# A decoder trunk on one Trainium2 core: first loads held and reordered, last product in three parts

## The chip, the cores and the metric

The kernel runs on one core of one Trainium2 chip. A core has a matrix engine (TensorE, PE in the profile; its weight loads are listed apart as PEld), a vector engine (VectorE, DVE), a scalar engine (ScalarE, ACT), a general engine (GpSimd, POOL) and a synchronisation engine (SyncE, SP), each with a queue of its own that it works through in order. Transfers between HBM and the on-chip memory SBUF are issued from an engine's queue (here SP's, after the change ACT's too) and carried out by 16 DMA engines. Matrix products land in PSUM, eight banks of 128 x 512 32-bit numbers.

The metric is the device time of one execution in microseconds (us), lower is better, given as the median over several runs.

## What is computed

Two decoder layers on a sequence of 256 tokens with width 2048, all in 32-bit floating point. Layer 0 mixes tokens with 16-head attention that carries a forget gate, layer 1 with dilated windows; each layer ends with an MLP of width 8192. Cut to what matters here:

```
for i in range(2):
    h = rms_norm(x, mix_norm_g[i])                      # y = x * rsqrt(mean(x*x) + eps) * g
    x = x + (fox_attention(h, ...) if i == 0 else dilated_attention(h, ...))
    h = rms_norm(x, mlp_norm_g[i])
    x = x + (relu(h @ mlp_w_up[i]) ** 2) @ mlp_w_down[i]
return x

def fox_attention(h, w_in, b_f, q_gain, k_gain, w_out):
    q, k, v, f = split(h @ w_in)                        # w_in is 2048 x (3*2048 + 16)
    ...
```

## The kernel before

**Tiles.** x lies in SBUF as four tiles `xt[n]` (x0 to x3 in the trace, L142) of 128 partitions x 2 token blocks x 512 columns, 512 KB each. Weights come in pieces of 256 rows x 512 columns, also 512 KB: `load` (L252) issues one transfer into a `raw` tile (5 buffers), `split` (L268) turns it into two tiles, `wh` (ACT copies it into the matrix engine's reduced 32-bit format, L279) and `wl` (DVE subtracts that copy from the original, L280), 5 buffers each. So every weight piece costs one transfer, one ACT cast and one DVE subtraction.

**Products.** `product` (L297) multiplies the normalised activations with one 2048 x 512 block of weights, 16 steps over the depth (k), for two blocks of 128 tokens. Each step is three passes per token block: `wh` with the high part of the activations (L308), `wl` with the high part (L309), `wh` with the low part (L310). Two steps use up one weight piece, so a block is eight pieces and 96 passes of 512 columns. After each piece `split` is called for the piece five further on.

**The norm.** The gain g of the norm is applied when x is transposed: `norm_chain` (L356) transposes four 128 x 128 blocks of x on PE into a PSUM tile `ptx` (L365), ACT writes `hT` = ptx times gain (L370), DVE writes the low part (L371). The factor rsqrt(mean) is put in after the product; its sum of squares is taken by ACT (`junk`, L381). The gains themselves are loaded as rows (`g_mix`, L128), transposed on PE and copied by DVE into `gain` (L135, L136).

**The start.** SP issues, in this order: the gains' rows, x0 in two halves of 256 columns for both token blocks, the weight pieces 0 and 1, x1, the pieces 2 and 3, x2, piece 4, x3, the gate's weights `wf` (2048 rows of 64 bytes, L160), and so on. PE begins with eight transposes of an identity matrix into an unused tile (`wake(8)`, L116), then transposes the gains and x0, then twelve more of the idle transposes (`wake(12)`), then the first product (q of heads 0 to 3). After it stand the gate's 32 passes (`pf`, L520), and the second product (k of heads 0 to 3). In the second product stand `pft` (L536) and `pc` (L565), small products of the gate's chain, which runs for the rest on DVE and ACT.

**What sets the order.** `Jobs` (L41) is a hand-made planner: a generator that yields a number waits for so many steps over k ("ticks"). `norm_chain` gets two such numbers, `wait` before its transposes and `later` before its sums of squares. `behind(...)` (L243) only places instructions after others in the order of issue; a real wait comes from the data (a semaphore).

**The end.** The last product adds `acc * rstd * rstd` to x on DVE per token block (`add_chain`, L687, L692), and `store` (L705) sends 256 KB for each from SP's queue.

```
        acc = [ps_acc.tile([P, NC], F32, tag="acc", name=f"acc{used[0]}_{t}") for t in range(NT)]
        for k in range(KC):
            ...
            for t in range(NT):
                ...
                nc.tensor.matmul(acc[t], ah[:, tok], hi, start=first, stop=False)
                nc.tensor.matmul(acc[t], ah[:, tok], lo, start=False, stop=False)
                issued["product"] = nc.tensor.matmul(acc[t], al[:, tok], hi, start=False, stop=last)
```

Of the kernel before, what the change touches and what calls it, by code (L numbers as in the profile page):

```python
# [9 lines left out]
F32 = mybir.dt.float32  # L10
# [3 lines left out]
ALU = mybir.AluOpType  # L14
# [3 lines left out]
P = 128  # L18
D = 2048
S = 256  # L20
NT = S // P
# [66 lines left out]
def trunk(ctx: ExitStack, tc, x, fox_w_in, fox_b_f, fox_q_gain, fox_k_gain, fox_w_out, dil_w_in,  # L88
# [68 lines left out]
    def more_constants():  # L157
        yield 6
        wf = work.tile([P, KC, FH], F32, tag="t2", name="wf")
        nc.sync.dma_start(wf, fox_w_in[0][:, 3 * D:3 * D + FH].rearrange("(c p) n -> p c n", p=P))  # L160
        nc.sync.dma_start(bf, fox_b_f.to_broadcast([P, FH]))
        qk_rows = gain_rows("g_qk", [fox_q_gain, fox_k_gain, dil_q_gain[0], dil_k_gain[0]])
        mlp_rows = gain_rows("g_mlp", [mlp_norm_g.rearrange(per_chunk, p=P)])
        di = distances()
# [78 lines left out]
    def behind(*instructions):  # L243
# [3 lines left out]
        return stack  # L247

    state = {"raw": 0, "split": 0}
    raws, splits = [], []  # L250

    def load():  # L252
        i = state["raw"]
        if i >= len(plan):
            return
        w, r, cols = plan[i]
        t = wpool.tile([P, RAW_SUB, NC], F32, tag="raw", name=f"raw{i}", bufs=RAW_BUFS)
        at = 0
        for c, width in cols:
            nc.sync.dma_start(  # L260
                t[:, :, at:at + width],
                w[r:r + RAW_SUB * P, c:c + width].rearrange("(c p) n -> p c n", p=P),
            )
            at += width
        raws.append(t)
        state["raw"] += 1

    def split():  # L268
        i = state["split"]
        per = RAW_SUB // W_SUB  # L270
        if i >= len(plan) * per:
            return
        if i % per == 0:
            load()
        raw = raws[i // per][:, (i % per) * W_SUB:(i % per + 1) * W_SUB, :]
        hi = wpool.tile([P, W_SUB, NC], F32R, tag="wh", name=f"wh{i}", bufs=W_BUFS)
        lo = wpool.tile([P, W_SUB, NC], F32R, tag="wl", name=f"wl{i}", bufs=W_BUFS)
        with behind(*(issued.get("n0", []) if i < 2 * W_BUFS else [])):
            nc.scalar.copy(hi, raw)  # L279
            nc.vector.tensor_sub(lo, raw, hi.bitcast(F32))  # L280
        splits.append((hi, lo))
# [15 lines left out]
    def product(keys, lhs, post):  # L297

        acc = [ps_acc.tile([P, NC], F32, tag="acc", name=f"acc{used[0]}_{t}") for t in range(NT)]
        for k in range(KC):  # L300
# [13 lines left out]
            jobs.tick()  # L314
        jobs.spawn(post(acc))

    def product_transposed(keys, both, banks, post):
# [38 lines left out]
    def norm_chain(tag, col, n, ssp, wait, later):  # L356
        yield wait
        for half in range(2):
            pr = n * 2 + half
            pt = ps_tp.tile([P, 2, S], F32, tag="tp", name=f"ptx_{tag}_{pr}")  # L360
            with behind(*([issued["product"]] if wait else [])):
                for i in range(2):
# [12 lines left out]
            jobs.done.add((tag, pr))  # L375
            yield min(wait, 1)
        yield later
        with behind(issued[tag, n * 2 + 1][0]):
            for t in range(NT):
# [307 lines left out]
    def add_chain(acc, n, then, ready, scale):  # L687
# [11 lines left out]
        yield 0  # L699

    def out_proj(keys, lhs, then=None, ready=None, scale=None):
        for n in range(NX):
            product(keys, lhs, lambda acc, n=n: add_chain(acc, n, then, ready, scale))

# [48 lines left out]

    first = normed("n0", 0, lambda n: (0, 1, 4, 8)[n], lambda n: 11 - 3 * n)

    def load_x(n):
        step = NC if n else NC // 2
        for c in range(0, NC, step):
            nc.sync.dma_start(xt[n][:, :, c:c + step], xv[:, :, n * NC + c:n * NC + c + step])

    def rest():
        load_x(2)
        yield 2
        split()
        load_x(3)
        while state["split"] - used[0] < W_BUFS:
            split()
            yield 1

    load_x(0)  # L770
    gain_columns("g_mix", mix_rows, 0)
    jobs.spawn(first(0))
    with behind(issued["transposed"]):
        wake(12)
    for i in range(4):
        split()
        if i == 1:
            load_x(1)
    for n in range(1, NX):
# [64 lines left out]
```

## Time and profile before

| | |
|---|---|
| median of three runs | 2198.79 us (2198.11 to 2200.05) |
| the profiled execution, its own time | 2198.39 us |
| span of its trace, first to last instruction | 2196.7 us |
| DVE / ACT busy | 1373.5 us / 1099.4 us |
| transfers from HBM | 421.70 MB, 193 GB/s over the span |
| x stored at the end | 8 transfers of 256 KB, median 5.5 us from issue to landing |

The lines of a timeline read: start in us from the span's start, duration, engine, line of the kernel, operation, written tile <- read tiles, shapes, number of merged instructions, and in brackets the idle time of that engine just before and what ended it. Names of tiles stand without buffer numbers. "SPq" is the work of SP's queue, here the issue of transfers, not the transfer itself. A duration of a PE row includes its pipeline's latency; how fast passes follow one another is read from the distance of their starts.

### The profile page before, as it was taken

To read this page: it belongs to the slowest core of one execution; us is meant where nothing else is said; L and a number is where in the kernel's file an instruction comes from. 1 tells how busy PE (TensorE), PEld (TensorE's weight loads), DVE (VectorE), ACT (ScalarE), POOL (GpSimd) and SP (SyncE) were. 2 spreads that over 40 slices of the span, in tenths; PEclk is the share of its full clock that TensorE was granted. 3 is DMA by queue.
4 is the path that set the end of the run, shared out by engine and by line. 5 is a ranking of instruction groups with operands and counts; after the bars stand their busy time and mean duration, and the time that the engine had idled before them with its cause. 6 is when DMAs were issued, how large, how long until landed. Compare 5 with 4: busy or idle time off the path is not lost.

```text
span 2196.7 us, 29876 instructions
## 1 busy us (share of the span) xinstructions
PE 2182.1 (99%) x11441; PEld 1938.2 (88%) x11441; DVE 1373.5 (63%) x1799; ACT 1099.4 (50%) x1516; POOL 48.2 (2%) x51
## 2 busy tenths in 40 slices
PE   8999999999999999999999999999999999999999
PEld 7888888998998998998888888888988988988988
DVE  6776686665565565565666766765655665665564
ACT  5555555554454454455555555555544544544442
POOL 1011000000000000000000000000000000000000
PEclk9999999999999999999999999999999999999999
DMA  7566545666666666665665565655656656656664
GB/s 233 163 184 179 177 170 196 197 202 203 202 201 203 202 202 204 201 202 194 192 190 182 173 192 172 193 173 192 202 204 203 202 203 204 200 203 202 201 211 143
DMA packets 248688, 425.76 MB, mean 194 GB/s; under 512 B 16793, under 2 KB 66529, under 8 KB 248545
## 3 DMA queue, kind: packets, MB, share of 16 engines
q1 hardware_dynamic: 248544, 423.86, 60.6%
q8 instruction: 89, 1.46, 0.3%
q14 instruction: 55, 0.44, 0.1%
HBM read 421.70 MB, written 2.10 MB: 193 GB/s over the span
## 4 chain that ended last, share of the span: by engine, by line
PE 95%; ACT 2%; DVE 2%; issue 1%; DMA 0%; SPq 0%; DVEq 0%; ACTq 0%
PE acc L310 20%; PE acc L308 20%; PE acc L309 20%; PE up_n3a_acc L329 5%; PE up_n1a_acc L329 5%; PE up_n3a_sc L329 3%; PE up_n1a_tp L329 3%; PE up_n3a_tp L329 3%; PE up_n1a_sc L329 3%; PE up_n1a_acc L333 3%; PE up_n3a_acc L333 3%; PE up_n1a_sc L333 1%; PE up_n3a_tp L333 1%; PE up_n1a_tp L333 1%; PE up_n3a_sc L333 1%; ACT wh L279 1%
## 5 line engine op out<-in xcount | busy, mean ns | idle before, releaser
L280 DVE TENSOR_TENSOR wl<-raw,wh 128x1024 fp32r<-128x1024 f32 x800 | 978.9, 1224 | 715.4 <-ACT wh L279 710.4
L279 ACT CAST wh<-raw 128x1024 fp32r<-128x1024 f32 x800 | 838.9, 1049 | 901.8 <-PE acc L310 546.3
L308 PE MATMUL acc<-wh,hT_n 128*128 128x512 f32 x896 | 346.2, 387 | 0.0
L309 PE MATMUL acc<-wl,hT_n 128*128 128x512 f32 x896 | 340.2, 380 | 0.0
L310 PE MATMUL acc<-wh,hT_n 128*128 128x512 f32 x896 | 339.8, 379 | 0.0
L308 PE MATMUL acc<-wh,aTh_n1a 128*128 128x512 f32 x512 | 194.5, 380 | 0.0
L309 PE MATMUL acc<-wl,aTh_n1a 128*128 128x512 f32 x512 | 194.0, 379 | 0.0
L310 PE MATMUL acc<-wh,aTl_n1a 128*128 128x512 f32 x512 | 194.0, 379 | 0.0
L308 PE MATMUL acc<-wh,aTh_n3a 128*128 128x512 f32 x512 | 194.0, 379 | 0.0
L309 PE MATMUL acc<-wl,aTh_n3a 128*128 128x512 f32 x512 | 194.0, 379 | 0.0
L310 PE MATMUL acc<-wh,aTl_n3a 128*128 128x512 f32 x512 | 194.0, 379 | 0.0
L310 PEld LDWEIGHTS acc<-wh,hT_n 128*128 128x128 f32 x896 | 169.4, 189 | 23.6
L308 PEld LDWEIGHTS acc<-wh,hT_n 128*128 128x128 f32 x896 | 169.6, 189 | 21.9 <-ACT wh L279 0.4
L309 PEld LDWEIGHTS acc<-wl,hT_n 128*128 128x128 f32 x896 | 169.6, 189 | 21.6 <-DVE wl L280 0.8
L329 PE MATMUL up_n3a_acc<-hT_n,wh 128*128 128x512 f32 x512 | 181.6, 382 | 0.0
L329 PE MATMUL up_n1a_acc<-hT_n,wh 128*128 128x512 f32 x512 | 181.6, 382 | 0.0
L333 PE MATMUL up_n3a_acc<-hT_n,wl 128*128 128x256 f32 x512 | 139.6, 273 | 0.0
L333 PE MATMUL up_n1a_acc<-hT_n,wl 128*128 128x256 f32 x512 | 139.6, 273 | 0.0
L309 PEld LDWEIGHTS acc<-wl,aTh_n3a 128*128 128x128 f32 x512 | 96.8, 189 | 13.8
L310 PEld LDWEIGHTS acc<-wh,aTl_n1a 128*128 128x128 f32 x512 | 96.8, 189 | 13.7
L310 PEld LDWEIGHTS acc<-wh,aTl_n3a 128*128 128x128 f32 x512 | 96.8, 189 | 13.7
L308 PEld LDWEIGHTS acc<-wh,aTh_n3a 128*128 128x128 f32 x512 | 96.8, 189 | 13.6
(721 smaller groups left out, 3159.9 us busy)
## 6 DMA issues: line engine op xcount, KB each, us to landing
raw<-in_mlp_w_up_dram SPq DMA_DIRECT2D x256, 512.0 KB, 4.3
raw<-in_mlp_w_down_dram SPq DMA_DIRECT2D x256, 512.0 KB, 3.9
raw<-in_fox_w_in_dram SPq DMA_DIRECT2D x96, 512.0 KB, 3.8
raw<-in_dil_w_in_dram SPq DMA_DIRECT2D x192, 256.0 KB, 3.0
raw<-in_fox_w_out_dram SPq DMA_DIRECT2D x32, 512.0 KB, 3.8
raw<-in_dil_w_in_dram SPq DMA_DIRECT2D x32, 512.0 KB, 3.6
raw<-in_dil_w_out_dram SPq DMA_DIRECT2D x32, 512.0 KB, 3.7
out_dram<-x SPq DMA_DIRECT2D x8, 256.0 KB, 5.5
```

Source lines behind the costliest of these rows:

```text
L279: nc.scalar.copy(hi, raw)
L280: nc.vector.tensor_sub(lo, raw, hi.bitcast(F32))
L308: nc.tensor.matmul(acc[t], ah[:, tok], hi, start=first, stop=False)
L309: nc.tensor.matmul(acc[t], ah[:, tok], lo, start=False, stop=False)
L310: issued["product"] = nc.tensor.matmul(acc[t], al[:, tok], hi, start=False, stop=last)
L329: issued["product"] = nc.tensor.matmul(banks[b], hi[:, i, col], in_turn(tokens.rearrange("p x s -> p (x s)"), P // 2), start=first, stop=last)
L333: nc.tensor.matmul(banks[b][:, 0:S], lo[:, i, col], in_turn(tokens[:, 0, :], P // 2), start=False, stop=False)
```

## The change

- x0 is loaded in two pieces by token block (whole rows of 512 columns) instead of two pieces by columns.
- Weight piece 0 is loaded in two halves from ACT's queue.
- The pieces 1 to 4 and x1 to x3 are issued in the order piece 1, x1, piece 2, x2, piece 3, x3, piece 4. Each is held by a small DVE memset into its destination, which is placed behind the copy that writes `gain`; so the transfer has to wait for that memset.
- Piece 0 is cast and subtracted in two halves, ahead of the first `hT`.
- Only x0's first two chunks are transposed before the first product; the second two stand inside it. `wake(12)` becomes `wake(6)`.
- The gate's weights, its bias and the other gains are loaded later, behind the last weight load; the sums of squares of the first norm are taken later (`later` is 13, 11, 9, 7 instead of 11, 8, 5, 2).
- In all norms, the sums of squares are placed behind the last cast issued, instead of behind the norm's last `hT`.
- The very last product (`last_product`) has three accumulators: token block 0 with 512 columns, token block 1 with 256 columns twice. For k below 8 the three take turns; then each runs its remaining steps alone, one after the other, and is added to x and stored as soon as it is done, the last one from ACT's queue.

```diff
     def more_constants():
-        yield 6
+        yield 9
         wf = work.tile([P, KC, FH], F32, tag="t2", name="wf")
-        nc.sync.dma_start(wf, fox_w_in[0][:, 3 * D:3 * D + FH].rearrange("(c p) n -> p c n", p=P))
-        nc.sync.dma_start(bf, fox_b_f.to_broadcast([P, FH]))
-        qk_rows = gain_rows("g_qk", [fox_q_gain, fox_k_gain, dil_q_gain[0], dil_k_gain[0]])
-        mlp_rows = gain_rows("g_mlp", [mlp_norm_g.rearrange(per_chunk, p=P)])
+        with behind(issued["load"]):
+            nc.sync.dma_start(wf, fox_w_in[0][:, 3 * D:3 * D + FH].rearrange("(c p) n -> p c n", p=P))
+            nc.sync.dma_start(bf, fox_b_f.to_broadcast([P, FH]))
+            qk_rows = gain_rows("g_qk", [fox_q_gain, fox_k_gain, dil_q_gain[0], dil_k_gain[0]])
+            mlp_rows = gain_rows("g_mlp", [mlp_norm_g.rearrange(per_chunk, p=P)])
...
+    def hold(first):
+        if "held" not in issued:
+            return ExitStack()
+        with behind(*issued["held"]):
+            nc.vector.memset(first, 0.0)
+        return behind(issued["load"])
...
-            nc.sync.dma_start(
-                t[:, :, at:at + width],
-                w[r:r + RAW_SUB * P, c:c + width].rearrange("(c p) n -> p c n", p=P),
-            )
+            src = w[r:r + RAW_SUB * P, c:c + width].rearrange("(c p) n -> p c n", p=P)
+            if i:
+                with hold(t[:, 0, 0:1]):
+                    issued["load"] = nc.sync.dma_start(t[:, :, at:at + width], src)
+            else:
+                for part in range(RAW_SUB):
+                    nc.scalar.dma_start(t[:, part, at:at + width], src[:, part, :])
...
-        if i % per == 0:
+        if i % per == 0 and state["raw"] <= i // per:
             load()
...
-        with behind(*(issued.get("n0", []) if i < 2 * W_BUFS else [])):
-            nc.scalar.copy(hi, raw)
-            nc.vector.tensor_sub(lo, raw, hi.bitcast(F32))
+        with behind(*([issued["gained"]] if i == 0 else issued.get("n0", []) if i < 2 * W_BUFS else [])):
+            for part in ([slice(0, 1), slice(1, 2)] if i < 1 else [slice(0, W_SUB)]):
+                issued["cast"] = nc.scalar.copy(hi[:, part, :], raw[:, part, :])
+                nc.vector.tensor_sub(lo[:, part, :], raw[:, part, :], hi[:, part, :].bitcast(F32))
...
+    def last_product(keys, lhs, ready):
+        parts = [(0, slice(0, NC)), (1, slice(0, S)), (1, slice(S, NC))]
+        acc = [ps_acc.tile([P, NC], F32, tag="acc", name=f"last{x}") for x in range(len(parts))]
+        begin = used[0]
+        steps = [(k, x) for k in range(KC // 2) for x in range(len(parts))]
+        steps += [(k, x) for x in range(len(parts)) for k in range(KC // 2, KC)]
+        for k, x in steps:
+            jobs.need(keys(k))
+            t, cols = parts[x]
+            hi, lo = (in_turn(w[:, k % W_SUB, :])[:, 0, cols.start // 2:cols.stop // 2, :]
+                      for w in splits[begin + k // W_SUB])
+            ah, al = lhs(k)
+            tok = slice(t * P, (t + 1) * P)
+            first, last = k == 0, k == KC - 1
+            to = acc[x][:, 0:cols.stop - cols.start]
+            nc.tensor.matmul(to, ah[:, tok], hi, start=first, stop=False)
+            nc.tensor.matmul(to, ah[:, tok], lo, start=False, stop=False)
+            nc.tensor.matmul(to, al[:, tok], hi, start=False, stop=last)
+            if last:
+                ready(to, t, cols)
+            if k < KC // 2 and x == len(parts) - 1:
+                if k % W_SUB == W_SUB - 1:
+                    split()
+                jobs.tick()
...
-            with behind(*([issued["product"]] if wait else [])):
+            with behind(*([issued["product"]] if "product" in issued else [])):
...
-            yield min(wait, 1)
+            yield 1
         yield later
-        with behind(issued[tag, n * 2 + 1][0]):
+        with behind(issued["cast"]):
...
+    def final_add(n, tag):
+        def ready(acc, t, cols):
+            at = halves(xt[n][:, t, :])[:, 0, :, cols.start // 2:cols.stop // 2]
+            sums = acc.rearrange("p (n h) -> p h n", h=2)
+            nc.vector.scalar_tensor_tensor(at, sums, rstd[tag, 2][:, t:t + 1], at, ALU.mult, ALU.add)
+            dst = out[0][t * P:(t + 1) * P, n * NC:(n + 1) * NC].rearrange("p (h n) -> p h n", h=2)
+            (nc.scalar if cols.start else nc.sync).dma_start(dst[:, :, cols.start // 2:cols.stop // 2], at)
+        return ready
+
     def out_proj(keys, lhs, then=None, ready=None, scale=None):
         for n in range(NX):
+            if ready is not None and n == NX - 1:
+                last_product(keys, lhs, final_add(n, scale))
+                continue
...
-    first = normed("n0", 0, lambda n: (0, 1, 4, 8)[n], lambda n: 11 - 3 * n)
+    first = normed("n0", 0, lambda n: (0, 2, 6, 10)[n], lambda n: (13, 11, 9, 7)[n])
 
     def load_x(n):
-        step = NC if n else NC // 2
-        for c in range(0, NC, step):
-            nc.sync.dma_start(xt[n][:, :, c:c + step], xv[:, :, n * NC + c:n * NC + c + step])
+        for t in range(NT) if n == 0 else [slice(0, NT)]:
+            with hold(xt[n][:, 0, 0:1]):
+                issued["load"] = nc.sync.dma_start(xt[n][:, t, :], xv[:, t, n * NC:(n + 1) * NC])
 
     def rest():
-        load_x(2)
-        yield 2
-        split()
-        load_x(3)
         while state["split"] - used[0] < W_BUFS:
             split()
             yield 1
 
     load_x(0)
-    gain_columns("g_mix", mix_rows, 0)
+    load()
+    gained = gain_columns("g_mix", mix_rows, 0)
+
+    issued["gained"] = gained
+    issued["held"] = [gained]
+    for what in (load, lambda: load_x(1), load, lambda: load_x(2), load, lambda: load_x(3), load):
+        what()
+    del issued["held"]
     jobs.spawn(first(0))
     with behind(issued["transposed"]):
-        wake(12)
-    for i in range(4):
-        split()
-        if i == 1:
-            load_x(1)
+        wake(6)
+    split()
     for n in range(1, NX):
         jobs.spawn(first(n))
     jobs.spawn(rest())
```

## The prediction, made before the changed kernel ran

> **What bounds the kernel now.** I read the page first, then the timeline of the start engine by engine, the busy times by stretch, and the end.
>
> ```profile
> span 2196.7 us, 29876 instructions
> PE 2182.1 (99%) x11441; PEld 1938.2 (88%) x11441; DVE 1373.5 (63%) x1799; ACT 1099.4 (50%) x1516; POOL 48.2 (2%) x51
> PE 95%; ACT 2%; DVE 2%; issue 1%; DMA 0%; SPq 0%; DVEq 0%; ACTq 0%
> ```
>
> The matrix engine is busy 99% of the time and carries 95% of the chain that ended last. It has only a start, a tail and a few stalls to give. The order in which both kernels are built shows that the change moves instructions before about 60 us and in the last product; between them only some sums of squares change places on ACT. So I reckon from the span's start to the first pass of the second product, and then the tail. SP's queue, PE and ACT at the start:
>
> ```profile
> 0.80 0.39 SPq L128 DMA_DIRECT2D g_mix<-in_mix_norm_g_dram  x1
> 1.25 0.93 SPq L759 DMA_DIRECT2D x<-in_x_dram  x2
> 2.22 0.98 SPq L260 DMA_DIRECT2D raw<-in_fox_w_in_dram  x2
> ...
> 8.39 0.79 SPq L160 DMA_DIRECT2D wf<-in_fox_w_in_dram  x1
> ```
>
> ```profile
> 4.07 1.11 PE L365 MATMUL ptx_n<-ident,x 128*128 128x128 f32 x4
> 6.77 1.09 PE L365 MATMUL ptx_n<-ident,x 128*128 128x128 f32 x4 [1.58 <-DMA x<-in_x_dram]
> 7.65 2.77 PE L116 MATMUL spare<-ident 128*128 128x128 f32 x12
> 10.38 1.22 PE L308 MATMUL acc<-wh,hT_n 128*128 128x512 f32 x2
> 11.64 0.52 PE L309 MATMUL acc<-wl,hT_n 128*128 128x512 f32 x1
> ...
> 12.64 0.60 PE L365 MATMUL ptx_n<-ident,x 128*128 128x128 f32 x4
> ```
>
> ```profile
> 2.09 0.20 ACT L105 ACTIVATE warm<-warm 128x1 f32<-128x1 f32 x1
> ...
> 12.46 1.05 ACT L279 CAST wh<-raw 128x1024 fp32r<-128x1024 f32 x1 [1.19 <-DMA raw<-in_fox_w_in_dram]
> 13.82 1.05 ACT L279 CAST wh<-raw 128x1024 fp32r<-128x1024 f32 x1 [0.32 <-DMA raw<-in_fox_w_in_dram]
> 14.78 0.47 ACT L370 ACTIVATE hT_n<-ptx_n,gain 128x256 fp32r<-128x256 f32 x1
> ...
> 21.74 1.04 ACT L279 CAST wh<-raw 128x1024 fp32r<-128x1024 f32 x1 [3.23 <-DMA raw<-in_fox_w_in_dram]
> ```
>
> The first product begins at 10.38. Two casts wait for pieces 2 and 3 until 12.46 and 13.82: one 512 KB transfer follows another in 1.36 us. Back from there in such steps, x1 landed at 11.1, piece 1 at 9.74, piece 0 at 8.38; x0's halves released PE at 4.07 and 6.77. So loads decide the start. The stretch behind it, and the passes that bound it:
>
> ```profile
> 10.37:42.81 32.44, 29.30 (x155) 24.01 (x155) 24.26 (x41) 22.83 (x43) 1.30 (x3) 1.00 0.89 273
> ```
>
> ```profile
> 27.11 0.63 PE L365 MATMUL ptx_n<-ident,x 128*128 128x128 f32 x4 [2.67 <-issue]
> ...
> 39.10 3.87 PE L520 MATMUL pf<-hT_n,wfs 128*32 128x256 f32 x32
> 42.81 0.38 PE L308 MATMUL acc<-wh,hT_n 128*128 128x512 f32 x1
> 43.03 0.38 PE L309 MATMUL acc<-wl,hT_n 128*128 128x512 f32 x1
> 43.24 0.38 PE L310 MATMUL acc<-wh,hT_n 128*128 128x512 f32 x1
> ```
>
> The second product begins at 42.81, 32.4 us after the first; PE's first figure, 29.30, is its busy time. The work in it: 96 passes at 0.2157 (42.81 to 43.24 are two steps) = 20.7; six groups of four transposes at 4 x 0.11 = 2.6 (0.60 less a latency of 0.27, over three steps); two small transposes of gains, estimated at 0.33 each beside such a group's 0.44; the gate 42.81 - 39.10 = 3.7. Together 27.7, so 4.7 us are stalls, some inside passes that the busy time counts. The largest is the 2.67 before 27.11. ACT stood there in its order: the cast of piece 5 at 21.74 had waited 3.23 for its load, and the high parts of x2 came behind it and the next cast. That load stood in SP's queue behind x3 and the gate's weights of 8.39.
>
> **The change, part by part.**
>
> *First loads.* Wanted first are x0 and the first half of piece 0. ACT issues that half at about 0.8, as its first instruction, the second half behind the table load and the warm-up, with an issue (0.39 as at 0.80) in front: 2.09 + 0.20 + 0.39 = 2.7. x0's first half before took 4.07 - 1.25 = 2.82 from issue to use. Its second piece is issued half of 0.93 later, at 1.72, and so wanted at 4.54; with the half piece of weights between, 1.36 / 2 = 0.68 more: 5.2. Bounds: 4.4 if ACT's transfer costs x0 nothing, and 7.2 if both pass as slowly as the first megabyte before (8.38, less 0.68 for the half not needed and 0.45 for the earlier issue). I take 5.2, nearest to the row at 4.07; whole rows double what the first transposes wait for.
>
> The Trainium skill, DMA: Bandwidth & Descriptors, "Issuing engines are not separate DMA queues", says that transfers issued from several engines run on the same 16 DMA engines and interleave; by that rule the 0.68 is due. No run of before, which issues everything from SP, can show it.
>
> *First pass.* Four transposes from 5.2 at 0.21 apart (2.77 less a latency of about 0.4, over eleven steps) leave PE at 6.1; six idle ones add 1.3: 7.3. The other path is not later: second half of piece 0 at 2.7 + 2.82 = 5.5, half a cast of 1.05, and hT 0.47, which waits for the transposes' end at about 6.3: 6.8. So the first pass starts at 7.3 (6.4 to 9.4 by x0's bounds), 3.1 earlier.
>
> *Held loads.*
>
> ```profile
> 4.17 0.19 DVE L136 COPY gain<-ps_g_mix 128x32 f32<-128x32 f32 x1 [0.53 <-PE ps_g_mix L135]
> ```
>
> `gain` is written at 4.36. Seven memsets of one column follow on DVE, ahead of its first subtraction; the nearest row, the one-column warm-up on ACT, took 0.20, so at most 1.4 us, ended at 5.8, before the first half's cast is subtracted for a pass at 7.3. Piece 1 is issued at about 4.5; of the loads in the first 50 us
>
> ```profile
> DMA to landing us min/median/max: 3.7/6.1/10.0
> ```
>
> the quickest took 3.7, so it lands at 8.2 (before 9.74), the next ones 1.36 apart: x1 9.6, piece 2 10.9, x2 12.3, piece 3 13.6, x3 15.0, piece 4 16.4, piece 5 17.7. PE needs 24 x 0.2157 + 0.88 = 6.1 us for one x tile and two pieces, the transfers 4.1, so loads stay ahead. Only piece 1 is tight: cast 1.05 and a subtraction of about as much behind 8.2, with an hT between, end at 11 to 11.5; PE wants them at 7.3 + 12 x 0.2157 + 0.44 = 10.3 at full pace. Piece 5 comes four us before the old 21.74, since the gate's weights now stand behind piece 8 (they are wanted only by the gate), so the 2.67 should go. Work to the second product's start is 20.7 + 7 x 0.44 (x0's second group now lies inside) + 0.33 + 3.7 = 27.8; the other gains' transpose moves into the second product, 0.3.
>
> *Pace.* Passes don't run at full speed at first. Four transposes took 1.11 and 1.09 early and 0.60 at 12.64; the two passes at 10.38 took 1.22. The granted-clock column says 1.00 in that stretch, so only durations show it; the turn lies near 11.7. If it comes after as much work without a break as before (6.77 to 11.7, 4.9 us), it falls at 5.2 + 4.9 = 10.1, and 10.1 - 7.3 at half pace costs 1.4. Ends: 0.4 (turn at 8.1) and 2.2 (turn at 11.7). With piece 1's wait of up to 0.8, partly in the same time, I put in 1.7 (0.9 to 3.0).
>
> Second product's start: 7.3 + 27.8 + 1.7 + 0.3 = 37.1 against 42.81: 5.7 gained.
>
> *Second product.*
>
> ```profile
> PE pc L565 <- DVE g_lf L562: 0.9, 1, 0.9
> ```
>
> `pc` waited 0.9 for the gate's chain on DVE. In the new order it stands 89 passes into that product, 19 us, instead of 54; the chain stands behind a subtraction whose buffer PE frees 17 passes, 3.7 us, earlier, time enough for a cast and a subtraction. The last sums of squares come behind a cast that PE frees 12 passes (2.6 us) in, and the product that needs them first starts 20 us in. I take 0.8 (0 to 1.0).
>
> *Tail.*
>
> ```profile
> 101.72 0.27 PE L469 MATMUL po_f<-pTh_f,fv0h 128*128 128x256 f32 x1
> 101.83 0.28 PE L469 MATMUL po_f<-pTl_f,fv0h 128*128 128x256 f32 x1
> 101.94 0.28 PE L469 MATMUL po_f<-pTh_f,fv0l 128*128 128x256 f32 x1
> ```
>
> ```profile
> 2192.13 1.41 DVE L692 SCALAR_TENSOR_TENSOR x<-acc,rstd_n,x 128x512 f32<-128x512 f32 x2 [10.00 <-PE acc L310]
> ...
> 2192.36 0.38 PE L310 MATMUL acc<-wh,aTl_n3a 128*128 128x512 f32 x1
> 2192.91 0.99 SPq L706 DMA_DIRECT2D out_dram<-x  x2
> ```
>
> ```profile
> L371 DVE SCALAR_TENSOR_TENSOR hT_n<-ptx_n,gain,hT_n 128x256 fp32r<-128x256 f32 x64 | 30.3, 482 | 16.2 <-ACT hT_n L370 15.8
> ```
>
> From the last pass's start to the span's end are 4.3 us: 0.38, the second of two additions of 0.70 on DVE, the store's issue and landing. After it: a 256-column pass ends 0.10 sooner; the addition takes 0.48 at most, as this row of 256 columns (-0.25), and starts free of the one before (-0.05); the store has half the bytes in twice as many pieces (0, from -0.2 to +0.3). Against it 96 passes at 0.11 stand for 48 at 0.2157: +0.2. Net -0.2 (-0.6 to +0.3). The casts of its last pieces are issued before the second half of k, so the quicker use of pieces there finds them ready; the third accumulator's buffer is freed by an addition about 0.4 before it is wanted.
>
> **Sum.** 5.7 + 0.8 + 0.2 = 6.7 off the profiled execution's 2198.39 (span and 1.7 around it), which lies 0.40 under the median of the runs: 2191.7 there, 2192.1 as a median.
>
> **The rivals.**
>
> *Two queues hold each other up.* x0 lands at its upper bound 7.2, the first pass starts at 9.4; the turn of pace then costs 1.2 and piece 1's wait is mostly inside it. Second start 9.4 + 27.8 + 1.3 + 0.3 = 38.8, gain 4.0 + 0.8 + 0.2 = 5.0: 2193.8. For it: x0's second half was wanted from 5.2 and came at 6.77, beside the first weights. Against: the weights' bytes in front are half as many now.
>
> *The pace turns late*, at 15.0, one such stretch of 4.9 later, for want of six idle transposes: (15.0 - 7.3) / 2 = 3.9 for 1.7; gain 6.7 - 2.2 = 4.5: 2194.3. For it: the transposes of 4.07 left those of 6.77 as slow. Against: a stretch of 4.9 without a break did bring it, and the new one breaks at most for piece 1.
>
> The Trainium skill, TensorE: Matmul & The Clock Gate, "What's actually happening", says that the array runs at half rate until one window of about 3.4 us, free-running against the kernel's start, was busy. By that the turn would fall anywhere from 8.6 to 12.0, and the sum between 2191.4 and 2193.1.
>
> *The large stall isn't one of loads.* If ACT's order keeps the 2.67, the gain is 4.0: 2194.8. For it: the row at 27.11 names "issue", no DMA. Against: the 3.23 before the cast at 21.74. That is also how the change would not do what it says.
>
> *Slower: 256-column passes.* If long rows of them, each with its own weights, go no quicker than 512-column ones, 96 x (0.2157 - 0.1079) = 10.3 is lost in the last product: 2192.1 + 10.3 = 2202.4. It decides from a pace of 0.18 on (6.7 / 96 above 0.108). For it: the rows at 101.72 are three in a row, not 48. Against: they follow at 0.11.
>
> **How the numbers follow.** Forecast 0.62; queues 0.14; late pace 0.08; stall stays 0.10; slow passes 0.04; 0.02 for what I don't see. Likeliest: 2192.1. The forecast's good ends (6.4, 0.9, 1.0, 0.6: another 0.9 + 0.8 + 0.2 + 0.4) give 2189.8, the stall that stays with the forecast's worst pace 2194.8 + 1.3 = 2196.1: range 2189.5 to 2196.0. About 0.2%, 4.4 us, can be told from no change, so faster means below 2194.4: the forecast, most of the queues' case and half of the late pace, 0.78; same 0.18; slower 0.04.
>
> **What would show it.** Right: first pass near 7.3, the second product's first near 37, no PE wait over 1 us between nor before `pc`, 256-column passes 0.11 apart, 4.0 from the last pass to the end. Wrong: transposes of x0 after 7, a cast of pieces 2 to 6 waiting for a load, passes of 0.5 and more after 12, or a last product over 21.5 us.

## The result, and the profile after

| | before | after |
|---|---|---|
| median of 10 runs each | 2199.21 us (2197.89 to 2200.16) | 2193.14 us (2192.83 to 2194.21) |
| ratio to before, 95% interval | | 0.9975 (0.9965 to 0.9984) |
| profiled execution, its own time | 2198.39 us | 2193.07 us |
| first pass, first pass of the second product, of the third | 10.38, 42.81, 66.83 | 8.45, 37.79, 61.54 |

The change takes 6.1 us off the median, 5.3 off the profiled execution. Matrix engine and chain are as full as before; the page of the kernel after:

```profile
span 2191.4 us, 29975 instructions
PE 2180.2 (99%) x11483; PEld 1938.7 (88%) x11483; DVE 1373.2 (63%) x1808; ACT 1101.0 (50%) x1517; POOL 48.0 (2%) x51
PE 95%; ACT 2%; DVE 2%; issue 1%; DMA 0%; POOL 0%; SPq 0%; ACTq 0%; DVEq 0%; POOLq 0%
```

What moved lies in the first 40 us. The timeline of ACT and its queue, then of DVE, after:

```profile
0.80 0.42 ACTq L276 DMA_DIRECT2D raw<-in_fox_w_in_dram  x1
1.25 1.28 ACT L105 ACT_TABLE_LOAD   x1 [1.25 <-PEq L883]
1.32 0.38 ACTq L276 DMA_DIRECT2D raw<-in_fox_w_in_dram  x1
...
4.64 0.62 ACT L293 CAST wh<-raw 128x512 fp32r<-128x512 f32 x1 [1.89 <-DMA raw<-in_fox_w_in_dram]
5.91 0.62 ACT L293 CAST wh<-raw 128x512 fp32r<-128x512 f32 x1 [0.65 <-DMA raw<-in_fox_w_in_dram]
7.55 0.48 ACT L411 ACTIVATE hT_n<-ptx_n,gain 128x256 fp32r<-128x256 f32 x1 [1.02 <-PE ptx_n L406]
...
11.09 0.48 ACT L411 ACTIVATE hT_n<-ptx_n,gain 128x256 fp32r<-128x256 f32 x1 [2.03 <-PE ptx_n L406]
11.46 1.04 ACT L293 CAST wh<-raw 128x1024 fp32r<-128x1024 f32 x1
```

```profile
4.36 0.19 DVE L136 COPY gain<-ps_g_mix 128x32 f32<-128x32 f32 x1 [0.71 <-PE ps_g_mix L135]
4.50 0.06 DVE L255 MEMSET raw<- 128x1 f32 x1
...
4.55 0.06 DVE L255 MEMSET raw<- 128x1 f32 x1
```

ACT issues the second half of piece 0 at 1.32, while its table load runs from 1.25 to 2.53. Piece 0's halves are cast at 4.64 and 5.91; no later cast of the first product waits for a transfer (the one at 11.46 stands behind an `hT` that waits for PE). The seven memsets take 0.11 us together. PE, after:

```profile
5.68 0.47 PE L406 MATMUL ptx_n<-ident,x 128*128 128x128 f32 x1 [1.36 <-DMA x<-in_x_dram]
6.61 0.90 PE L406 MATMUL ptx_n<-ident,x 128*128 128x128 f32 x3 [0.45 <-DMA x<-in_x_dram]
7.31 1.49 PE L116 MATMUL spare<-ident 128*128 128x128 f32 x6
8.45 0.78 PE L322 MATMUL acc<-wh,hT_n 128*128 128x512 f32 x1
9.01 0.63 PE L323 MATMUL acc<-wl,hT_n 128*128 128x512 f32 x1
9.44 0.53 PE L322 MATMUL acc<-wh,hT_n 128*128 128x512 f32 x1
9.80 0.38 PE L323 MATMUL acc<-wl,hT_n 128*128 128x512 f32 x1
...
12.55 0.70 PE L322 MATMUL acc<-wh,hT_n 128*128 128x512 f32 x2 [0.20 <-ACT wh L293]
...
37.79 0.38 PE L322 MATMUL acc<-wh,hT_n 128*128 128x512 f32 x1
```

x0's pieces release PE at 5.68 and 6.61. The first pass stands at 8.45, three steps of 0.36 to 0.57 follow, and from about 9.7 passes run 0.22 apart. Between 14 and 37.79 no step is more than 0.12 over its pitch: the 2.67 before 27.11 is gone. From the list of PE's waits (in total, times, longest) the row of `pc`, and then the end of PE and DVE:

```profile
PE pc L606 <- DVE g_lf L603: 0.2, 1, 0.2
```

```profile
2166.74 0.38 PE L348 MATMUL last<-wh,aTh_n3a 128*128 128x512 f32 x1
...
2187.59 0.28 PE L349 MATMUL last<-wl,aTh_n3a 128*128 128x256 f32 x1
2187.71 0.28 PE L350 MATMUL last<-wh,aTl_n3a 128*128 128x256 f32 x1
2188.02 0.48 DVE L746 SCALAR_TENSOR_TENSOR x<-last,rstd_n,x 128x256 f32<-128x256 f32 x1 [2.20 <-PE last L350]
```

`pc` waits 0.2 where it had waited 0.9. The 256-column passes follow 0.11 apart, and from the last pass's start to the span's end are 3.7 us for 4.3.

### The profile page after: what moved, and what is told of

The parts are those of the page before. It is cut to its first block, busy times and chain, and to the rows that moved or that the text cites. A ratio compares the mean times of both kernels' runs of the same rounds, so it can differ in the third digit from the quotient of the medians.

```text
span 2191.4 us, 29975 instructions
## 1 busy us (share of the span) xinstructions
PE 2180.2 (99%) x11483; PEld 1938.7 (88%) x11483; DVE 1373.2 (63%) x1808; ACT 1101.0 (50%) x1517; POOL 48.0 (2%) x51
## 4 chain that ended last, share of the span: by engine, by line
PE 95%; ACT 2%; DVE 2%; issue 1%; DMA 0%; POOL 0%; SPq 0%; ACTq 0%; DVEq 0%; POOLq 0%
PE acc L323 20%; PE acc L324 20%; PE acc L322 20%; PE up_n1a_acc L370 5%; PE up_n3a_acc L370 5%; PE up_n1a_tp L370 3%; PE up_n3a_sc L370 3%; PE up_n3a_tp L370 3%; PE up_n1a_sc L370 3%; PE up_n3a_acc L374 3%; PE up_n1a_acc L374 3%; PE up_n1a_sc L374 1%; PE up_n3a_sc L374 1%; PE up_n3a_tp L374 1%; PE up_n1a_tp L374 1%
## 5 line engine op out<-in xcount | busy, mean ns | idle before, releaser
L294 DVE TENSOR_TENSOR wl<-raw,wh 128x1024 fp32r<-128x1024 f32 (+1 forms) x801 | 979.5, 1223 | 708.8 <-ACT wh L293 703.1
L293 ACT CAST wh<-raw 128x1024 fp32r<-128x1024 f32 (+1 forms) x801 | 839.9, 1049 | 895.2 <-PE acc L324 546.0
L322 PE MATMUL acc<-wh,aTh_n3a 128*128 128x512 f32 x480 | 181.9, 379 | 0.0
L323 PE MATMUL acc<-wl,aTh_n3a 128*128 128x512 f32 x480 | 181.9, 379 | 0.0
L324 PE MATMUL acc<-wh,aTl_n3a 128*128 128x512 f32 x480 | 181.9, 379 | 0.0
L323 PEld LDWEIGHTS acc<-wl,aTh_n1a 128*128 128x128 f32 x512 | 96.8, 189 | 13.6
L322 PEld LDWEIGHTS acc<-wh,aTh_n1a 128*128 128x128 f32 x512 | 96.8, 189 | 13.5
L370 PEld LDWEIGHTS up_n3a_acc<-hT_n,wh 128*128 128x128 f32 x512 | 96.8, 189 | 13.5
```

The costliest lines, as they stand in the source:

```text
L293: issued["cast"] = nc.scalar.copy(hi[:, part, :], raw[:, part, :])
L294: nc.vector.tensor_sub(lo[:, part, :], raw[:, part, :], hi[:, part, :].bitcast(F32))
L370: issued["product"] = nc.tensor.matmul(banks[b], hi[:, i, col], in_turn(tokens.rearrange("p x s -> p (x s)"), P // 2), start=first, stop=last)
```

## The experiments

Twelve kernels. Stages are read from their profiles, since a part is worth less than two medians can tell apart; each profile is one execution. Medians stand with the ratio to before of the same runs. "Second product" with a time means the start of its first pass. Two start from the kernel before, ten from the changed one.

**The stall: loads or ACT's order?** Two parts of the change, each alone on the kernel before.

```diff
-        yield 6
+        yield 9
         wf = work.tile([P, KC, FH], F32, tag="t2", name="wf")
...
+        with behind(issued["load"]):
```

> The kernel before, with one part of the change: the gate's weights, bias and the other gains are issued behind the last weight load (planner step 9 for 6). ACT's order is that of before. Theory (the stall of 2.67 before 27.11 is one of loads): 2048 rows of 64 bytes stand in SP's queue ahead of piece 5, whose cast waited 3.23 until 21.74; without them piece 5 lands about 2.4 earlier, at 19.3 (piece 3 at 13.82 and four more transfers of 1.36); that cast waits under 1.2, the stall on PE is under 0.7, and the second product starts at 40.0 to 40.7 for 42.81. Rival (ACT's own order keeps the stall: sums of squares between the high parts): the stall stays above 2.0 and the second product starts after 42.2.

```diff
-            nc.scalar.copy(hi, raw)
+            issued["cast"] = nc.scalar.copy(hi, raw)
...
-        with behind(issued[tag, n * 2 + 1][0]):
+        with behind(issued["cast"]):
...
-    first = normed("n0", 0, lambda n: (0, 1, 4, 8)[n], lambda n: 11 - 3 * n)
+    first = normed("n0", 0, lambda n: (0, 1, 4, 8)[n], lambda n: (13, 11, 9, 7)[n])
```

> The kernel before, with one other part of the change: the sums of squares of the first norm are taken later (13, 11, 9, 7 for 11, 8, 5, 2) and stand behind the last cast; the loads stay in their old order. Theory (stall of loads): piece 5's cast still waits about 3 us until 21.7; the stall keeps 1.3 or more, since only the two sums of 0.73 each between the high parts after 24.07 go from the chain; second product no earlier than 41.2. Rival (ACT's order): the stall falls under 0.7 and the second product starts before 40.7, with piece 5 as late as before.

The gate's weights moved alone: ACT's cast of piece 5, and PE at the place of the stall:

```profile
19.44 1.05 ACT L280 CAST wh<-raw 128x1024 fp32r<-128x1024 f32 x1 [0.80 <-DMA raw<-in_fox_w_in_dram]
```

```profile
24.80 0.63 PE L366 MATMUL ptx_n<-ident,x 128*128 128x128 f32 x4 [0.22 <-PE acc L311]
```

The cast comes at 19.44 for 21.74 and waits 0.80 for 3.23; PE waits 0.22 where it had waited 2.67. Second product 40.05 for 42.81; median 2195.76 (2195.37 to 2196.32), ratio 0.9985 (0.9975 to 0.9994). The sums moved alone: the same cast, and PE:

```profile
21.23 1.04 ACT L279 CAST wh<-raw 128x1024 fp32r<-128x1024 f32 x1 [3.24 <-DMA raw<-in_fox_w_in_dram]
```

```profile
26.45 0.63 PE L365 MATMUL ptx_n<-ident,x 128*128 128x128 f32 x4 [2.51 <-issue]
...
27.75 0.63 PE L308 MATMUL acc<-wh,hT_n 128*128 128x512 f32 x1
28.18 0.63 PE L309 MATMUL acc<-wl,hT_n 128*128 128x512 f32 x1
```

The stall stays, the second product starts at 43.83, and the median is 2201.51 (2199.08 to 2202.51), ratio 1.0009 (1.0000 to 1.0019). The theory of loads holds and the rival falls: the gate's weights ahead of piece 5 make the stall. The passes of 0.43 behind it were not expected; more on them below.

These two runs also show how far two single executions can lie apart. Their first pass came at 9.65 and 9.15, for 10.38, and all eight transposes of x0 ran in one go from 4.92 and 4.66, though SP's issues up to 5.3 are the same: in the profile of the kernel before, x0's second half was waited for until 6.77, here it was there at least 1.0 earlier. From the first pass to the second product are 30.4 (gate's weights moved) and 34.7 (sums moved) for 32.4.

**x0: who holds it up?** Back to halves by columns, the rest as changed:

```diff
-        for t in range(NT) if n == 0 else [slice(0, NT)]:
+        step = NC if n else NC // 2
+        for c in range(0, NC, step):
             with hold(xt[n][:, 0, 0:1]):
-                issued["load"] = nc.sync.dma_start(xt[n][:, t, :], xv[:, t, n * NC:(n + 1) * NC])
+                issued["load"] = nc.sync.dma_start(xt[n][:, :, c:c + step], xv[:, :, n * NC + c:n * NC + c + step])
```

> The changed kernel with x0 in two halves of 256 columns, as before, everything else as changed. Theory (the first transposes wait for x0's bytes, and whole rows double what they wait for): all four transposes have run by 5.5, the first half lands at 4.1 to 4.8, and the first pass then waits for the second half of piece 0 (cast at 5.91, then the high part 0.48): 6.8 to 7.4 for 8.45. If the turn of pace stays at 9.7, the passes moved ahead of it run at half speed: second product 37.0 (36.4 to 37.3) for 37.79. Rival (the two queues hold each other up, whatever is asked for first): x0's first half comes at 6 or later and the first pass after 8.0; second product at 37.6 to 38.2.

PE of this run, and the two queues' packets from 1.0 to 4.6 (q10 is ACT's; packets, MB, share of 16 engines):

```profile
6.20 1.11 PE L406 MATMUL ptx_n<-ident,x 128*128 128x128 f32 x4 [2.07 <-DMA x<-in_x_dram]
...
8.25 0.77 PE L322 MATMUL acc<-wh,hT_n 128*128 128x512 f32 x1
```

```profile
q10 hardware_dynamic: 220, 0.42, 41.0%
q1 hardware_dynamic: 219, 0.19, 22.1%
```

The theory falls: the first transposes need 256 KB for 512 KB, and have them at 6.20, not much before whole rows (6.61) and later than the first row piece of the same 256 KB (5.68). The packets point to why: up to 4.6 the queues had 220 and 219 (32 of SP's are small ones of the gains), as if they took turns packet by packet, and SP's packets of 1 KB then carry half of what ACT's of 2 KB do. With whole rows the counts over the same stretch are 220 and 181, and SP moved 0.28 MB for 0.19. That is the rival's mechanism. In time it makes no difference that these runs can tell: the first pass stands at 8.25 for 8.45, and the median, 2193.05, is that of the changed kernel. That the second product started at 38.74, later than the rival's 37.6 to 38.2, goes with a pace that turned only at about 12.0, and this profile is of the slowest of the nine executions (2193.93).

Then piece 0 held like the other pieces, so that x0 has the engines to itself, and piece 0 behind x0 in SP's queue:

```diff
+                with behind(issued["gained"]):
+                    nc.vector.memset(t[:, :, 0:1], 0.0)
                 for part in range(RAW_SUB):
                     nc.scalar.dma_start(t[:, part, at:at + width], src[:, part, :])
...
     load_x(0)
+    gained = gain_columns("g_mix", mix_rows, 0)
+    issued["gained"] = gained
     load()
-    gained = gain_columns("g_mix", mix_rows, 0)
```

> The changed kernel with piece 0 held by a memset as the other pieces are, so that ACT issues it only after 4.4 and x0 has the DMA engines nearly to itself. Theory (the transfers of both queues share the engines): x0's second piece releases PE at 5.2 (4.5 to 5.6) for 6.55; piece 0 lands at 7.5 to 9, the first pass is at 9 to 10.5, and the second product starts 0.8 to 1.8 later than 37.79. Rival (the first transfers are slow by themselves, whatever runs beside them): x0's second piece is still wanted until 6.3 to 6.8.

```diff
-                    nc.scalar.dma_start(t[:, part, at:at + width], src[:, part, :])
+                    issued["load"] = nc.sync.dma_start(t[:, part, at:at + width], src[:, part, :])
```

> The changed kernel with piece 0's two halves issued by SP right behind x0, none by ACT. Theory (two queues take turns packet by packet, one queue serves in order): x0's second piece releases PE at 4.6 to 5.2, as it did at 4.89 when piece 0 was held back, for 6.61 as changed; piece 0's halves then come at 5.3 to 6.0 and 6.1 to 6.8, since the same megabyte has to pass; first pass 7.6 to 8.3. Rival (ACT's queue brings transfers that SP's alone would not carry): x0 lands early too, but piece 0's second half lands after 7.5 and the first pass is after 8.9.

PE with piece 0 held, then with piece 0 on SP:

```profile
4.89 0.90 PE L408 MATMUL ptx_n<-ident,x 128*128 128x128 f32 x3 [0.22 <-DMA x<-in_x_dram]
...
9.29 1.22 PE L324 MATMUL acc<-wh,hT_n 128*128 128x512 f32 x2 [2.23 <-ACT wh L295]
```

```profile
5.15 0.90 PE L406 MATMUL ptx_n<-ident,x 128*128 128x128 f32 x3 [0.43 <-DMA x<-in_x_dram]
...
7.88 0.80 PE L322 MATMUL acc<-wh,hT_n 128*128 128x512 f32 x1 [0.54 <-ACT hT_n L411]
...
13.16 0.63 PE L323 MATMUL acc<-wl,hT_n 128*128 128x512 f32 x1
```

x0's second piece comes at 4.89 and 5.15 for 6.61: for x0 both theories hold. ACT's 512 KB beside it cost x0 1.5 to 1.7 us. This is more than one execution's chance: the run with the old tail, whose start is that of the changed kernel, has 6.48, and in the two later runs with x0's rows and piece 0 on SP no transpose of x0 waits after 4.97. With piece 0 held, the first pass comes at 9.29 and the second product at 39.72, as that theory said or 0.1 later. On SP piece 0 was cast from 6.20, a little later than forecast, and the first pass is earlier, 7.88, yet the second product starts at 38.87: PE rested 0.54 before the first pass and passes ran 0.43 apart until 13.6, so 0.6 gained became 1.1 lost in this execution, the slowest of its eight (2194.07). Medians 2194.81 (piece 0 held; ratio 0.9982, 0.9972 to 0.9991) and 2193.65 (on SP; 0.9976, 0.9965 to 0.9986).

**Is the hold worth its memsets?** A return ahead of the memset leaves it out:

```diff
             return ExitStack()
+        return behind(issued["load"])
         with behind(*issued["held"]):
             nc.vector.memset(first, 0.0)
```

> The changed kernel without the seven memsets: the same loads in the same order, but none held until the gain is written. Theory (x0 stands ahead of them in SP's queue, so only ACT's second half has more to share with): x0's pieces release PE at 5.4 to 6.8 as before, piece 0's second half is cast at 6.0 to 7.0 for 5.91, the first pass is at 8.4 to 9.2, and piece 1's earlier landing brings nothing, since its cast stands behind an hT on ACT; second product at 37.6 to 38.4. Rival (the hold is what makes the start quick): piece 0's second half comes after 7.5, the first pass after 9.5, second product 38.6 or later.

```profile
7.68 0.90 PE L407 MATMUL ptx_n<-ident,x 128*128 128x128 f32 x3 [0.46 <-DMA x<-in_x_dram]
...
9.52 0.78 PE L323 MATMUL acc<-wh,hT_n 128*128 128x512 f32 x1
```

The rival holds, by another way than it says: x0 itself comes at 7.68 for 6.61, though all the unheld loads stand behind it in SP's queue; piece 0's second half is cast at 6.97. First pass 9.52, second product 40.45, 2.7 later than with the hold; 1.1 of this lies ahead of the first pass, and about 1.0 in two waits for DVE's low parts, before 25.43 and 31.66. Median 2195.30, ratio 0.9982 (0.9972 to 0.9992).

**The tail.** The last product, its addition and its stores as before:

```diff
-            if ready is not None and n == NX - 1:
-                last_product(keys, lhs, final_add(n, scale))
-                continue
```

> The changed kernel with the last product, its addition and its stores as before. Theory (the parts shorten the tail): 4.2 to 4.5 from the last pass's start to the span's end, for 3.7 as changed and 4.3 before; the last product 0.2 shorter; in all 0.2 to 0.6 longer than the changed kernel. Rival (two queues and more pieces give back what the shorter addition saves): 3.8 or less, and no longer in all.

PE's first and last pass of the last product in this run (span 2192.0):

```profile
2167.21 0.38 PE L322 MATMUL acc<-wh,aTh_n3a 128*128 128x512 f32 x1
...
2187.72 0.38 PE L324 MATMUL acc<-wh,aTl_n3a 128*128 128x512 f32 x1
```

From the last pass to the end 4.3, as the theory says, for 3.7 with the parts; but the product, from its first pass to its last, is 20.51 for 20.97. From the first pass to the span's end 24.79 with the old tail and 24.66 with the new: 0.13 gained, less than the theory's 0.2 to 0.6. In the medians (2193.71 and 2193.14, ranges overlapping) it can't be seen.

**The pace.** Ten more idle transposes between the gains' and x0's:

```diff
+    wake(10)

     issued["gained"] = gained
```

> The changed kernel with ten more idle transposes between the gains' transpose and x0's, so that PE hardly rests between 1.9 and the first pass. Theory (the pace turns after PE has been busy for a stretch, and the idle 1.36 before 5.68 delays it): the turn comes before 8.7, all passes from the first at 8.45 run at full pace (0.22 apart; in the changed kernel three of them took 0.36 to 0.57), and the second product starts 0.5 to 0.9 earlier, at 36.9 to 37.3. Rival (idle transposes don't count, or the turn falls at a time of its own): passes of 0.42 and more remain until 9.7 or later, second product at 37.6 or later.

```profile
4.06 2.40 PE L116 MATMUL spare<-ident 128*128 128x128 f32 x10
6.25 1.15 PE L406 MATMUL ptx_n<-ident,x 128*128 128x128 f32 x4
7.22 0.83 PE L116 MATMUL spare<-ident 128*128 128x128 f32 x6
7.96 0.48 PE L322 MATMUL acc<-wh,hT_n 128*128 128x512 f32 x1
8.28 0.38 PE L323 MATMUL acc<-wl,hT_n 128*128 128x512 f32 x1
```

The theory holds, and more: the turn falls among the idle transposes of 7.22, so these end sooner, and the first pass comes earlier too, at 7.96. Second product 36.28; median 2191.76 (2191.53 to 2192.06), ratio 0.9968 (0.9957 to 0.9980): 1.4 below the changed kernel, and its runs lie within 0.5 for 1.4. On the same chip the run with the old tail, with its start as changed, took 2192.82 to 2194.32: the ranges don't meet.

**Earlier still?** Piece 0 on SP (the edit above), idle transposes in both places, ACT's first `hT` ahead of the casts; first with x0's rows, then with x0's columns and piece 0 between its halves:

```diff
+    wake(4)
...
-        wake(6)
+        wake(8)
...
-        with behind(*([issued["gained"]] if i == 0 else issued.get("n0", []) if i < 2 * W_BUFS else [])):
+        with behind(*([issued["hT0"]] if i == 0 else issued.get("n0", []) if i < 2 * W_BUFS else [])):
```

> The changed kernel with three edits: piece 0's halves issued by SP behind x0 (x0 wanted at 4.25 and 5.15 in the run that did only this), four idle transposes between the gains' transpose and x0's and eight for six behind them (PE hardly rests), and ACT writes the first high part ahead of piece 0's casts. Theory (what was late are piece 0's first half, cast at 6.20 there, and the turn of pace): first pass 6.9 to 7.4 at full pace; second product 0.6 to 1.2 earlier than the 36.28 of the run with ten idle transposes; median 2190.7 to 2191.3. Rival (piece 1, held until 4.4, is now late): a wait of 0.5 to 1.2 for piece 1's cast or subtraction after the twelfth pass, second product at 36.0 to 36.8, median 2191.5 to 2192.2.

> The same three edits, but x0 in halves of 256 columns with piece 0's halves issued between them (x0's first half, piece 0, x0's second half). Theory (the order of bytes in one queue decides): x0's first half at 4.0 to 4.6, piece 0's first half cast at 4.9 to 5.6, first pass 6.0 to 6.8; piece 1 then is late by 0.5 to 1.5; second product 35.2 to 36.2, median 2190.2 to 2191.5. Rival (1 KB pieces pass so slowly that the order brings nothing, as with x0's halves at 6.20 beside ACT's transfers): piece 0's first half after 6.2, first pass 7.2 or later, no better than the whole rows.

PE with the rows:

```profile
7.12 0.70 PE L322 MATMUL acc<-wh,hT_n 128*128 128x512 f32 x2 [0.20 <-ACT wh L293]
...
11.49 0.63 PE L406 MATMUL ptx_n<-ident,x 128*128 128x128 f32 x4 [0.78 <-DMA x<-in_x_dram]
```

The first pass comes at 7.12 and 7.39, and what is late next is x1: 0.78 and 0.97 of waiting at 11.49 and 11.75. Second product 36.49 and 37.27, medians 2192.01 (ratio 0.9967, 0.9955 to 0.9980) and 2191.94 (0.9965, 0.9952 to 0.9979). The rival of the first run holds in its sizes, with x1 late rather than piece 1; in the second, columns bring nothing over rows.

Last, the held loads let go 0.65 earlier, in the run with rows and in the one with ten idle transposes:

```diff
-    issued["held"] = [gained]
+    sel0 = make_sel(0)
+    issued["held"] = [issued["sel"]]
```

> The kernel with piece 0 behind x0 on SP, four and eight idle transposes and the first high part ahead of the casts, and the seven memsets now behind DVE's cast of sel (ended 3.64) instead of the copy of gain: the held loads go out about 0.65 earlier. Theory (from the first pass on, the held loads' landing sets the pace, and between 4.4 and the first held bytes the DMA engines stand half idle): piece 1's cast at 8.8 to 9.1 for 9.50, x1's transposes at 10.7 to 11.0 for 11.48, second product at 35.7 to 36.1 for 36.48, median 2191.2 to 2191.6. Rival (earlier loads hold up x0 and piece 0 by as much as they gain, as when nothing was held): x0's second piece after 5.6, first pass after 7.5, second product no earlier than 36.4.

> The changed kernel with ten more idle transposes ahead of x0's, and the memsets behind the cast of sel as in the other run. Theory (there piece 1's and x1's landings stop nothing any more, since the first pass comes at 7.96): nothing to gain; x0's second piece at 6.5 to 6.9, first pass 7.9 to 8.3, second product 36.2 to 36.7 for 36.28, median 2191.6 to 2192.3. Rival (earlier loads cost nothing and every landing counts): second product before 36.1, median under 2191.5.

PE and ACT of the first:

```profile
7.71 0.70 PE L322 MATMUL acc<-wh,hT_n 128*128 128x512 f32 x2 [0.80 <-ACT wh L293]
```

```profile
7.04 1.36 ACT L293 CAST wh<-raw 128x512 fp32r<-128x512 f32 x2 [0.49 <-DMA raw<-in_fox_w_in_dram]
```

x1 is no longer waited for, but piece 0 now comes later (cast at 7.04 for 6.46) and the first pass with it. Second product 36.38 and 36.77. In the first run the rival's times hold for the first pass and the second product, but not its way: x0 was not late, its transposes ran from 4.97 without a wait. The theory took the DMA engines to stand half idle from 4.4 on; in the run with rows they were 72% busy from 4.4 to 5.2 and full after that, which fits that the earlier loads took their share from piece 0. In the second run the theory holds, within 0.1. Medians 2191.63 (2191.39 to 2192.01; ratio 0.9963, 0.9949 to 0.9976) and 2191.99 (0.9965, 0.9952 to 0.9977). With PE kept busy, four of five ways of loading start the second product between 36.3 and 36.8: what one load gains, another gives back. All five have medians below the changed kernel's, at 2191.6 to 2192.0; which of them is best these runs can't decide.

## Why the prediction was right or wrong

**First loads: the step that failed.** x0's second piece was put at 5.2 and came at 6.61. Most of this is the term of 0.68 for half a piece in front, because the second half of piece 0 was taken to wait behind the table load until 2.7. It was issued at 1.32, so 512 KB took turns with x0's 512 KB: 1.7 for 0.68. The other 0.35 is x0 by itself, 4.89 with piece 0 held for the forecast's 4.54; the 2.82 that this rested on was one execution's, for in the two experiments on the kernel before x0's first half was wanted until 4.66 and 4.92 for 4.07. The mechanism is that of the rival "two queues hold each other up"; 6.61 lies between the forecast's 5.2 and the rival's 7.2. The rule cited from the Trainium skill, DMA: Bandwidth & Descriptors, "Issuing engines are not separate DMA queues", holds here. The Trainium skill, DMA: Bandwidth & Descriptors, "Queues, rings and completion order", says that each DMA engine goes round the queues it has work for, one packet at a time; the 220 and 219 packets agree, though what the profile counts as a packet may not be what that section calls one.

**First pass.** 8.45 for 7.3: 1.15 later, by the 1.4 of x0 less some slack. The other path (piece 0's second half, cast at 5.91) was indeed not later.

**Held loads.** Right that no piece from 2 on would be waited for. The memsets' price was over-bounded, 0.11 for 1.4. What the hold itself does was not priced: without it the second product starts 2.7 later (one execution each), and the median is 2.2 higher.

**Pace and piece 1.** 1.7 forecast; measured 0.6 (half of 8.45 to 9.7) and two waits for piece 1's cast and subtraction, before 12.55 and 13.81, that cost 0.4 each and with the slower step behind each 0.9 together: 1.6. The waits came from ACT's order, not from the landing. That the sum came out is luck in part, since the turn at 9.7, near the 10.1 forecast, was a draw. The run with the old tail has the same start (first pass 8.32); there passes ran 0.43 apart until about 11.1, and the second product came 0.5 later:

```profile
10.17 1.04 PE L324 MATMUL acc<-wh,hT_n 128*128 128x512 f32 x2
...
38.32 0.38 PE L322 MATMUL acc<-wh,hT_n 128*128 128x512 f32 x1
```

In the runs with x0's columns, piece 0 on SP, piece 0 held and nothing held the turn fell at about 12.0, 13.8, 14.3 and 13.0, 5 to 6 us after PE's last longer rest, against 3.1 with the changed kernel and 4.6 with the old tail. The forecast's "one stretch of 4.9" is one value of that spread. The free-running window of the Trainium skill (TensorE: Matmul & The Clock Gate, "What's actually happening"), cited there for a sum of 2191.4 to 2193.1, fits it better, since by it the same start can turn at different times, as here at 9.7 and 11.1.

**Work and the stall.** 27.7 of work (37.79 - 8.45 - 1.6) for 27.8. The stall went, and for the reason given: the gate's weights ahead of piece 5. The rival by which it would stay is refuted by the run that moved ACT's sums alone. The other gains' transpose was counted ahead of the second product, and lies in it (0.3).

**Second product.** The wait before `pc` fell by 0.7 (0.9 to 0.2) for 0.8. The time from the second to the third product fell by only 0.3 (24.02 to 23.75), since the gains' transpose went in (0.4).

**Tail.** Net -0.13 to -0.19 (24.66 from the last product's first pass to the end, for 24.79 and 24.85) for -0.2. Inside it both sides were too small: the end, from the last pass's start, 0.6 shorter for 0.4, the product, from its first pass to its last, 0.46 longer for 0.2. The forecast's own terms give -0.1, not -0.2: the 0.2 for 96 shorter passes already holds the 0.10 by which the last of them ends sooner, so this was counted twice. That the net came out is luck in part.

**Sum.** In the profiled execution 2193.07 for 2191.7. Of the 1.4 missing, 0.7 lie ahead of the second product (1.15 from the first pass, against 0.1 less of pace and waits, 0.1 less work and 0.3 of gains moved out), 0.5 inside it, and the rest behind. The median, 2193.14, is 1.0 over the forecast and well inside the range; the miss is smaller there because the forecast put the median 0.4 over the profiled execution, and it is only 0.1 over it.

For the kernel before, the median of ten runs is 0.8 over the profiled execution. That difference is part of the gain. Of 30 executions of before that ran beside the first four experiments, 10 had a mean granted clock of 1.000 and took 2197.6 to 2198.6; the other 20, with 0.998 or 0.999, took 2198.2 to 2200.2. The stall would explain it, as the granted clock (last but two) from 24 to 32 us suggests, first for the kernel before in its profiled execution, then with only the sums moved:

```profile
24.00:32.00 8.00, 5.33 (x30) 4.43 (x29) 6.97 (x13) 7.05 (x18) 0.20 (x1) 1.00 0.93 277
```

```profile
24.00:32.00 8.00, 5.55 (x22) 4.75 (x23) 7.24 (x14) 4.95 (x11) 0.20 (x1) 0.79 0.95 296
```

At 0.79 over 8 us, 3.4 us passed at half pace (0.21 x 8 / 0.5; passes 0.43 apart for 0.22), which costs 1.7; the medians of the two groups, 2198.2 and 2199.7, lie 1.5 apart. Without the stall (gate's weights moved alone) only 2 of 10 executions show 0.999, the runs lie within 1.0 for 2.6, and the median falls by 3.8 though the stall was 2.67. That the drop hits two of three executions of before is read from the mean clock alone: no profile of such an execution was taken, so this part is argued, not shown. The prediction had priced a stall at its own length.

## What to carry to other kernels

Before the first product, keep the matrix engine busy without a rest, with idle work if need be: in these runs the turn to full pace came 3 to 6 us after the last rest and at no fixed time, and a stall of 2.5 us in the middle cost another 1.7 in one profile, where one of 2.67 in another cost only itself. Order first loads by need, but let only what is needed first be in flight: 512 KB in another queue cost x0 1.5 to 1.7 us, and unheld loads behind it in its own queue another 1.1, and of two queues at work the one with smaller packets moved less (0.19 MB for 0.42). Loads of 64-byte rows belong behind everything that is waited for: here they cost a stall of 2.7. And compare single profiles of a start with care, since the same one came out 0.5 to 1 us apart.

## What the hardware showed that was not expected

- A stall of 2.51 us was enough to halve the pace, for 3.4 us (27.34 to 30.74 with the sums moved alone). The Trainium skill, TensorE: Matmul & The Clock Gate, "What's actually happening", asks for an idle window of about 3.4 us; the length of the half pace agrees with it, the idle time that it took does not. The 2.67 in the profiled execution of the kernel before was not followed by half pace (granted clock 1.00).
- ACT's queue issued a transfer at 1.32 while its table load, begun at 1.25, ran for 1.28.
- Loads behind x0 in x0's own queue delayed it by 1.1 us (7.68 for 6.61), with nothing but the seven memsets left out. With 512 KB alone behind it x0 came at 5.15, and at 4.89 with no weights issued before 4.4. By what way the loads behind it slow it is not shown.
